# The output product's right operands, split behind FFN 1 and kept in DRAM

## The chip, the cores and the metric

The kernel is written in Bass and Tile and runs on one core of one Trainium2 chip. The metric is the device time of one execution, in microseconds; 1917.81 us is the median of three runs before the change.

## The reference

One layer of a hybrid encoder trunk, in float32, on 1024 tokens of width 1024 (weights as one would expect; D_FF is 2816):

```python
h = x + 0.5 * swiglu(rms_norm(x, ffn1_norm), w_gate1, w_up1, w_down1)      # FFN 1
z = rms_norm(h, mix_norm) @ w_in                                           # input projection
qa, ka, va, qb, kb, vb, ga, gb = split(z)
ya = neighbourhood_attention_2d(qa, ka, va, na_rpb)
yb = windowed_gqa_sink(rope(qb), rope(kb), vb, sink_logit)
merged = sigmoid(ga) * (ya @ w_branch_a) + sigmoid(gb) * (yb @ w_branch_b)
h = h + merged @ w_out                                                     # output product
h = h + 0.5 * swiglu(rms_norm(h, ffn2_norm), w_gate2, w_up2, w_down2)      # FFN 2
return rms_norm(h, final_norm)
```

The change touches two places of it: the product `merged @ w_out` (1024 x 1024 x 1024), and work that is done in the background of FFN 1.

## The kernel before

**How a product is computed.** Every float32 operand is split into a high part, a cast to fp32r on ScalarE (ACT), and a low part, the difference to that, on VectorE (DVE). One product then is three matmuls: high x high, high x low, low x high (`mm3`, L146 to 153, with a matmul in each of the lines 149, 151 and 153). The large products use Strassen's scheme in Winograd's form: seven products of half-size blocks (`PRODUCTS`, named P1 to P7) take the place of eight, at the cost of block sums and differences, which DVE forms.

**The stages**, one after the other, as the trace has them: FFN 1's gate and up products and the multiplication of the two, `hid`, until about 433 us; its down product until about 650; the input projection; both attentions and the gates until about 1160; the last part of branch A, whose results are merged; the output product from about 1196, with the next normalization at its end; FFN 2 from about 1300.

**FFN 1** (`hidden`, L429) runs 154 units of 12 matmuls, 2.72 us each. A counter `n` goes down from 153 to 0, and `behind_ffn1(n)` (L770) is called at the end of unit `n`. For a column block `i` of the hidden width the products come in the order P1, P2, P5, P6, P7, P3, P4, each for gate (m = 0) and up (m = 1). In `after` (L446), P6 is copied out of PSUM by ACT (L477, a snapshot), and P7 is then accumulated on top of it in the same bank, so P7's first matmul needs P6's copy. The results of `hid` go to DRAM on GpSimd's queue (POOL, L444).

**The background of FFN 1** is work for later stages in the gaps of ACT and DVE. A list of 28 items (8 + 8 for the branch weights, kept in `wab_d`; 12 for six gate columns, kept in `wg_d`) goes through three steps: `wab_fetch` (L749, one load of 256 KB on SyncE's queue, SP), `wab_split` (L758; cast L760, subtraction L761) and `wab_put` (L764, two transfers of 256 KB on POOL's queue, L768). One item has three units: it is fetched at n = 100 - 3i, split two units later and put one unit after that; the last one is fetched at n = 19. All of it lives in the pool `hs` (L746): six slots of 128x512. Near the end of FFN 1, `down.at_end` (L607) starts the loads for the down product: block B11 of W_down at n = 10, the left operands at 7, block B21 at 6.

**The class `Down`** (L532) runs the two down products and the output product. Its entries are (product, p), for the output product 7 x 4 = 28, each of 12 matmuls. `prep` (L579) makes an entry's operands: the left one from DRAM or from `merged`, and the right one from blocks B11, B12, B21, B22 of the weight, which it combines in place (L590 to 595: one subtraction for P5 and P3, two for P6), and it splits both. The operands lie in a ring of slots: four pairs of the pool `ws` and, in the output product, two pairs in `ar` group 2 (`ring=(8, 10)`); `prep_until(e + RING)` runs ahead by up to six entries. The blocks of w_out, eight loads of 512 KB, are loaded by `load_blocks` in the loop over branch A's last part, at every second step.

**What sets the order.** Each engine has one queue in order. A scheduler orders each engine's instructions by priority when the program is built. Those that are marked with `pin` (`tc.keep_in_program_order`) keep the order in which they are written; the background's casts and subtractions are pinned, so are the casts of the output product (`late=True`).

Of the kernel before, what the change touches and what calls it, by code (L numbers as in the profile page):

```python
# [10 lines left out]
F32 = mybir.dt.float32  # L11
F32R = mybir.dt.float32r
AF = mybir.ActivationFunctionType
ALU = mybir.AluOpType

P = 128
T = 1024
D = 1024
NC8 = D // P
# [12 lines left out]
def f32v(ap):  # L32
    return ap.bitcast(F32)


@with_exitstack
def trunk_kernel(ctx, tc, x, xt, n1, wg1, wu1, wd1, nm, win, rpb, sink, wa, wb, wo,
                 n2, wg2, wu2, wd2, nf, c_rope, c_mask_a, c_mask_b, out):
    nc = tc.nc

# [9 lines left out]
    dram = ctx.enter_context(tc.tile_pool(name="dram", bufs=1, space=bass.MemoryType.DRAM))  # L50
# [3 lines left out]
    def nm_(s):  # L54
        uid[0] += 1
        return f"{s}_{uid[0]}"
# [16 lines left out]
    def new_ar(g, dt=F32R):  # L73
        ar[g] = main.tile([P, 4, 1024], dt, tag=f"ar{g}", bufs=1, name=nm_("ar"))
        return ar[g]

    def slot(k):
        return ar[k // 4][:, k % 4, :]
# [10 lines left out]
    def ws4():  # L89
        return main.tile([P, 1024], F32R, tag="ws", bufs=8, name=nm_("ws"))  # L90

    pin = tc.keep_in_program_order

    def split(dst_hi, dst_lo, src, eng=None, late=False):
        hi = nc.scalar.copy(dst_hi, src)  # L95
        if late:
            pin(hi)
        (eng or nc.vector).tensor_tensor(dst_lo, src, f32v(dst_hi), op=ALU.subtract)  # L98
# [56 lines left out]
    def drain(gen, n=1 << 30):  # L155

        for _ in range(n):
            if next(gen, gen) is gen:
                return

    def res(t):

        return fx[t] if t < 4 else fa[:, (t - 4) * 1024:(t - 3) * 1024]
# [23 lines left out]
    B11, B21, T2, T1, B22, T3, T4 = range(7)  # L187
# [47 lines left out]
    PRODUCTS = ("P1", "P2", "P5", "P6", "P7", "P3", "P4")  # L235
    RIGHT = dict(P1=B11, P2=B21, P6=T2, P5=T1, P7=T3, P3=B22, P4=T4)

    def products(src, n, after, at_end, extra, ring, by_hand=False, last=PRODUCTS, early_rooms=(), swapped=None):
# [144 lines left out]
        def prep_until(n):  # L383
            while done[0] < min(n, len(seq)):
                prep(done[0])
                done[0] += 1
# [135 lines left out]
    def pair_slots(s):  # L522
        return slot(s), slot(s + 1)
# [5 lines left out]

    SOURCE = dict(P1="B11", P2="B21", P5="B11", P6="B11", P3="B22", P7="B12", P4="B21")  # L530

    class Down:  # L532
# [2 lines left out]

        ORDER = ("P2", "P1", "P5", "P6", "P3", "P7", "P4")

        def __init__(self, n, w, scale, place, left=None, dram=None, loads={}, ring=(22, 24, 26), shift=0, late=False):
            self.n, self.w, self.scale, self.place, self.left, self.dram, self.loads = n, w, scale, place, left, dram, loads
            self.seq = [(k, p) for k in self.ORDER for p in range(n)]  # L540
            self.dk = [k for k in self.ORDER if k in dram]
            self.nd = (n + 1) // 2
            self.raw, self.nraw, self.done, self.ent, self.tiles, self.loaded = {}, 0, 0, {}, {}, {}
            self.TAIL, self.late = min(n, 5), late
            self.ring, self.shift, self.RING = ring, shift, 4 + len(ring)
            self.W = self.Y = None
# [32 lines left out]
        def prep(self, e):  # L579
            k, p = self.seq[e]  # L580
            if k in self.dram:
                d = self.dk.index(k) * self.nd + p // 2
                self.load_left(d + 3)
                left = self.raw[d][:, p % 2, :]
            else:
                left = self.left(k, p)
            b11, b12, b21, b22 = [self.blocks(n, p)[:, 0, :] if n in self.loaded else None for n in ("B11", "B12", "B21", "B22")]
            eng = nc.gpsimd if self.n > self.RING else nc.vector
            if k == "P5":
                nc.vector.tensor_tensor(b11, b12, b11, op=ALU.subtract)  # L590
            elif k == "P6":
                nc.vector.tensor_tensor(b11, b22, b11, op=ALU.subtract)
                eng.tensor_tensor(b12, b22, b12, op=ALU.subtract)
            elif k == "P3":
                eng.tensor_tensor(b21, b21, b11, op=ALU.subtract)
            i = (e + self.shift) % self.RING
            s, t = (ws4(), ws4()) if i < 4 else pair_slots(self.ring[i - 4])
            split(s[:, :512], s[:, 512:], left, None, self.late)
            split(t[:, :512], t[:, 512:], dict(B11=b11, B12=b12, B21=b21, B22=b22)[SOURCE[k]], None, self.late)
            self.ent[e] = s, t  # L600
# [74 lines left out]
    def down_ffn(wd, src):  # L675

        place = {n: [divmod(h0 + p, 8) for p in range(NP)] for n, h0 in (("B11", 0), ("B22", NP), ("B21", NP + 7), ("B12", 2 * NP + 7))}
        place["B22"][7:] = [(f"xs{k // 2}", k % 2) for k in range(4)]
        loads = {}
        for t in range(NTT):  # L680
            loads.setdefault(2 + t, []).append(lambda d, t=t: nc.sync.dma_start(res(t), src(t)))
        for name, e0 in (("B12", 8), ("B22", 19)):
            for a in range((NP + 1) // 2):
                loads.setdefault(e0 + a, []).append(lambda d, name=name: d.load_blocks(name, 2))
        return Down(NP, wd, 0.5, place, dram={k: hid[i] for i, k in enumerate(PRODUCTS)}, loads=loads)
# [8 lines left out]
    down = down_ffn(wd1[0], lambda t: x2[t])  # L694
# [47 lines left out]
    gates = [dc for dc in [*range(8, 16), *range(8)] if 18 + dc not in sum((p for g in groups for p in g), ())]  # L742
    wg_d = dram.tile([len(gates), 2, P, 1024], F32, name="wg_d")
    cast = {}

    def hs(dt):  # L746
        return main.tile([P, 512], dt, tag="hs", bufs=6, name=nm_("hs"))
# [16 lines left out]
    def wab_put(i):  # L764
        g, half = divmod(i - 2 * NC8, 2)
        for k, a in enumerate(cast.pop(i)):
            dst = wab_d[i, :, k * 512:k * 512 + 512] if g < 0 else wg_d[g, k, :, half * 512:half * 512 + 512]
            nc.gpsimd.dma_start(dst, f32v(a))  # L768

    def behind_ffn1(n):  # L770
        down.at_end(n)
        if n <= 60 and spread:
            nc.sync.dma_start(*spread.pop(0))
        for e, f in ((3, wab_put), (2, wab_split), (0, wab_fetch)):
            i, k = divmod(100 - e - n, 3)
            if k == 0 and 0 <= i < 2 * (NC8 + len(gates)):
                f(i)

    hg = hidden(wg1, wu1, behind_ffn1, (8, 10, 9, 11), by_hand=True)


# [371 lines left out]
    for c in range(5):  # L1153
        n = 14 * (NG - 1) - 8 - 6 * c
# [111 lines left out]
    def branch_a(i):  # L1266

        bs = [bank("dg"[i % 2]) for _ in range(2)]
        a_mm.append((bs, branch_mm(bs, mix.pop(("w", NC8 + i)), Y_A)))

    def merged(dc):
        return slot((0, 1, 2, 3, 24, 25, 26, 27)[dc])
# [40 lines left out]
    def a_fetch(i):  # L1313
        mix["ra", i] = raw4()
        nc.sync.dma_start(mix["ra", i], g_d[a_order[i] * P:(a_order[i] + 1) * P, :])

    def a_open(i):
        r = mix["ra", i]
        pin(nc.scalar.activation(r, r, AF.Tanh, scale=0.5))
# [191 lines left out]
    def load_h(t):  # L1511
        nc.sync.dma_start(res(t), h_d[t * P:(t + 1) * P, :])


    left_d = dram.tile([4, 4, P, 512], F32, name="left_d")

    def quarter(k, p):
        m = merged(p + (4 if k in ("P2", "P4") else 0))
        return m[:, :512] if k in ("P1", "P2") else m[:, 512:]

    place = dict(B11=[(4, p) for p in range(4)], B21=[(4, 4 + p) for p in range(4)],
                 B12=[(1, p) for p in range(4)], B22=[(1, 4 + p) for p in range(4)])
    loads = {t: [lambda d, t=t: load_h(t)] for t in range(NTT)}
    loads[0].append(lambda d: d.load_left(2))
    down = Down(4, wo[0], 0.5, place, quarter, {k: left_d[i] for i, k in enumerate(("P5", "P6", "P3", "P7"))},
                loads, (8, 10), late=True)

    def combine(p):
        a11, a12, a22 = [quarter(k, p) for k in ("P1", "P2", "P4")]
# [7 lines left out]
    for i, dc in enumerate(a_order):  # L1537
        r = mix.pop(("ra", i))
        if i + 2 < NC8:
            a_fetch(i + 2)  # L1540
        if i >= 2:
            branch_a(i)
        if i % 2 == 0:
            down.load_blocks(("B21", "B11", "B12", "B22")[i // 2])
        if i + 3 == NC8:
            new_ar(2)
        if i + 1 == NC8:
            down.prep_until(2)
        bs, mm = a_mm[i]
        drain(mm)  # L1550
        if i + 6 < NC8:
            fetch_w(NC8 + i + 6)
        if i + 2 < NC8:
            a_open(i + 2)
        for n in range(2):
            sl = slice(n * 512, (n + 1) * 512)
            nc.vector.scalar_tensor_tensor(out=r[:, sl], in0=r[:, sl], scalar=1.0, in1=bs[n], op0=ALU.add, op1=ALU.mult)
        nc.vector.tensor_tensor(merged(dc), merged(dc), r, op=ALU.add)
        if i % 2:
            combine(i // 2)  # L1560
# [4 lines left out]
    down = down_ffn(wd2[0], lambda t: h_d[t * P:(t + 1) * P, :])  # L1565
# [22 lines left out]
    late = {}  # L1588
# [111 lines left out]
```

## Time and profile before

| | |
|---|---|
| runs | 1917.64, 1917.81, 1918.79 us (median 1917.81) |
| profiled execution | span 1915.6 us from the first to the last instruction; its time is not listed apart from the runs, so the 2.2 us from the span to the median stand for what lies around the span |
| TensorE busy | 1905.7 us, 99% of the span, at a granted clock of 0.999 |
| VectorE, ScalarE, GpSimd busy | 1451.9, 947.5, 306.5 us |
| DMA | 338.57 MB, 177 GB/s over the span |
| output product, 1200 to 1250 us | TensorE 50.00 of 50 us busy, VectorE 49.88, DMA 216 and 106 GB/s |
| end of FFN 1, 400 to 450 us | TensorE 50.00 of 50 us busy, VectorE 30.50, DMA 335 and 387 GB/s |

Each instruction of the trace has an engine, a line of the program, an operation and the tile that it writes and reads (`fx<-g` writes `fx` from the PSUM bank `g`). Idle time ahead of an instruction is put down to what ended it (`<-PE d L153`). `L149`, `L151` and `L153` are the three matmuls of one product. "DMA to landing" is the time from the issue of a transfer until its data is there.

### The profile page before, as it was taken

The numbers are of one execution on the slowest core, as the hardware profiler recorded it, in microseconds if no ns is written. First come the engines' busy times: TensorE is split into PE (matmuls) and PEld (weight loads), VectorE is DVE, ScalarE is ACT, GpSimd is POOL, SyncE is SP. The second block draws the span as 40 slices with busy tenths as digits, with TensorE's granted clock in tenths as the row PEclk, the third lists the DMA queues.
The fourth block names the chain that finished last, engine by engine and source line by source line (L and its number), as shares of the span: only waits on it lengthen the run. The fifth ranks groups of instructions, "written<-read, shape, count | busy, mean of one in ns | idle before, by whom it ended". The sixth has DMA issues, their size and how long they took to land.

```text
span 1915.6 us, 25959 instructions
## 1 busy us (share of the span) xinstructions
PE 1905.7 (99%) x9044; PEld 1597.7 (83%) x9044; DVE 1451.9 (76%) x2545; ACT 947.5 (49%) x1847; POOL 306.5 (16%) x477
## 2 busy tenths in 40 slices
PE   9999999999999999999999999999999999999998
PEld 7888888888888888898898888888888888888886
DVE  8988766668967778755887997999675566569864
ACT  7533444444446543444888983475333333344453
POOL 0012222214400112211112201010110001005111
PEclk9999999999999999999999999999999999999999
DMA  7256656677354277753648978444432323492341
GB/s 269 95 175 217 231 200 219 205 277 284 115 180 141 105 213 236 226 176 127 176 117 228 283 225 309 171 154 133 142 110 97 118 88 110 157 357 86 119 140 61
DMA packets 174211, 338.57 MB, mean 177 GB/s; under 512 B 17280, under 2 KB 79616, under 8 KB 174080
## 3 DMA queue, kind: packets, MB, share of 16 engines
q1 hardware_dynamic: 140752, 235.18, 37.5%
q0 software_dynamic: 32464, 100.69, 15.6%
q8 instruction: 71, 1.16, 0.3%
q10 hardware_dynamic: 864, 1.05, 0.2%
q14 instruction: 60, 0.49, 0.1%
HBM read 230.43 MB, written 108.19 MB: 177 GB/s over the span
## 4 chain that ended last, share of the span: by engine, by line
PE 97%; DVE 1%; DMA 1%; ACT 0%; issue 0%; POOL 0%; SPq 0%; POOLq 0%; DVEq 0%; ACTq 0%
PE g L149 18%; PE g L153 17%; PE g L151 17%; PE d L153 12%; PE d L151 12%; PE d L149 12%; PE d L1438 2%; PE g L1457 1%; PE d L1417 1%; PE g L1452 1%; PE d L1418 1%; PE d L142 1%; DVE ar L98 0%; DMA fx<-in_xt_dram 0%; DMA fx<-v_d 0%
## 5 line engine op out<-in xcount | busy, mean ns | idle before, releaser
L149 PE MATMUL g<-ar,ws 128*128 128x512 f32 x1064 | 404.6, 393 | 0.0
L151 PE MATMUL g<-ar,ws 128*128 128x512 f32 x1064 | 401.8, 390 | 0.0
L153 PE MATMUL g<-ar,ws 128*128 128x512 f32 x1064 | 400.4, 390 | 0.0
L149 PE MATMUL d<-ar,ws 128*128 128x512 f32 x728 | 281.6, 390 | 0.4 <-ACT ar L908 0.4
L151 PE MATMUL d<-ar,ws 128*128 128x512 f32 x728 | 281.1, 389 | 0.6 <-DVE ar L910 0.6
L153 PE MATMUL d<-ar,ws 128*128 128x512 f32 x728 | 281.2, 389 | 0.0
L153 PEld LDWEIGHTS g<-ar,ws 128*128 128x128 f32 x1064 | 199.6, 188 | 41.6
L151 PEld LDWEIGHTS g<-ar,ws 128*128 128x128 f32 x1064 | 199.6, 188 | 41.0
L149 PEld LDWEIGHTS g<-ar,ws 128*128 128x128 f32 x1064 | 196.6, 188 | 35.9 <-DVE fa L1030 0.3
L332 DVE TENSOR_TENSOR ws<-raw,ws 128x512 fp32r<-128x512 f32 x216 | 147.6, 688 | 92.9 <-ACT ws L325 92.0
L325 ACT CAST ws<-raw 128x512 fp32r<-128x512 f32 x216 | 132.6, 620 | 149.6 <-PE g L153 67.0
L151 PEld LDWEIGHTS d<-ar,ws 128*128 128x128 f32 x728 | 136.7, 188 | 29.8 <-DVE ar L910 1.2
L149 PEld LDWEIGHTS d<-ar,ws 128*128 128x128 f32 x728 | 136.5, 188 | 28.9 <-ACT ar L908 0.9
L153 PEld LDWEIGHTS d<-ar,ws 128*128 128x128 f32 x728 | 136.6, 188 | 28.7 <-DVE ws L332 0.5
L95 ACT CAST ws<-raw 128x512 fp32r<-128x512 f32 x98 | 61.0, 623 | 119.2 <-PE d L153 59.9
L98 DVE TENSOR_TENSOR ws<-raw,ws 128x512 fp32r<-128x512 f32 x98 | 73.2, 747 | 44.3 <-ACT ws L95 44.2
L444 POOL DMA_DIRECT2D hid<-fx x91 | 49.2, 540 | 349.6 <-DVE fx L504 221.6
L98 DVE TENSOR_TENSOR ws<-ar,ws 128x512 fp32r<-128x512 f32 x114 | 93.5, 828 | 14.6 <-ACT ws L95 14.6
L95 ACT CAST ar<-raw 128x512 fp32r<-128x512 f32 (+1 forms) x81 | 54.0, 670 | 83.5 <-PE g L151 51.5
L149 PE MATMUL g<-ws,ws 128*128 128x512 f32 x232 | 90.9, 392 | 0.0
L153 PE MATMUL g<-ws,ws 128*128 128x512 f32 x232 | 90.4, 390 | 0.0
L151 PE MATMUL g<-ws,ws 128*128 128x512 f32 x232 | 90.3, 389 | 0.0
(344 smaller groups left out, 3830.9 us busy)
## 6 DMA issues: line engine op xcount, KB each, us to landing
raw<-hid SPq DMA_DIRECT2D x70, 512.0 KB
hid<-fx POOLq DMA_DIRECT2D x91, 256.0 KB, 2.7
ar<-in_ffn_w_down_dram SPq DMA_DIRECT2D x32, 512.0 KB
raw<-in_ffn_w_up_dram SPq DMA_DIRECT2D x31, 512.0 KB
raw<-in_ffn_w_gate_dram SPq DMA_DIRECT2D x27, 512.0 KB
hid<-fa POOLq DMA_DIRECT2D x51, 256.0 KB, 2.7
ar<-zs_d POOLq DMA_DIRECT2D x48, 256.0 KB, 7.5
raw<-in_w_in_dram SPq DMA_DIRECT2D x20, 512.0 KB
```

Of the source, the lines that this page charges most:

```text
L95: hi = nc.scalar.copy(dst_hi, src)
L98: (eng or nc.vector).tensor_tensor(dst_lo, src, f32v(dst_hi), op=ALU.subtract)
L142: nc.tensor.transpose(pt[:, c * P:(c + 1) * P], xs[:, (half * 4 + c) * P:(half * 4 + c + 1) * P], ident)
L149: nc.tensor.matmul(b, lhs[0], r[0], start=first, stop=False, **kw)
L151: nc.tensor.matmul(b, lhs[0], r[1], start=False, stop=False, **kw)
L153: nc.tensor.matmul(b, lhs[1], r[0], start=False, stop=last, **kw)
L325: nc.scalar.copy(w[0][:, :512], a)
L332: nc.vector.tensor_tensor(w[0][:, 512:], a, f32v(w[0][:, :512]), op=ALU.subtract)
L444: nc.gpsimd.dma_start(hid[PRODUCTS.index(p), i], src)
L1417: nc.tensor.matmul(b[:, :nw], un["q"][s], un["kd"][s][:, k0 * P:k1 * P], start=True, stop=False)
L1418: nc.tensor.matmul(b[:, :nw], un["q"][s], un["kl"][s][:, k0 * P:k1 * P], start=False, stop=True)
L1438: nc.tensor.transpose(pt[:, i * P:(i + 1) * P], un["pr"][s][:, i * P:(i + 1) * P], ident)
```

## The change

**The right operands of the output product** are no longer made in the output product. Three new functions do it behind FFN 1, for one p at a time: `wo_fetch` loads the four blocks of w_out for this p into four slots of `hs`, `wo_split` forms the difference that a product needs, in place, and splits it into two more slots of `hs`, and `wo_put` writes both to a new DRAM tensor `wo_d` (28 x 512 KB). A round has twelve units: p = 0 starts at n = 50, p = 1 at 38, p = 2 at 26, p = 3 at 14. The seven products follow at n0 - 0, 2, 3, 5, 6, 8, 9, in the order P2, P1, P3, P5, P7, P6, P4, each put one unit behind its split. The casts and subtractions are pinned.

In `Down.prep`, an entry with `right` set loads its high and low part from there by one transfer of 512 KB (L591) and only splits the left operand. The loads of w_out in the loop over branch A are gone.

**The list of 28 items** has now two units for an item: fetched at n = 108 - 2i, split at 106 - 2i, put at 105 - 2i, so that its last item is put at n = 51.

```diff
+            if self.right is not None:
+                i = (e + self.shift) % self.RING
+                s, t = (ws4(), ws4()) if i < 4 else pair_slots(self.ring[i - 4])
+                nc.sync.dma_start(f32v(t), self.right[PRODUCTS.index(k), p])
+                split(s[:, :512], s[:, 512:], left, None, self.late)
+                self.ent[e] = s, t
+                return
...
+    wo_d = dram.tile([len(PRODUCTS), 4, P, 1024], F32, name="wo_d")
+    wo = {}
+
+    def wo_fetch(p):
+        for n, (r0, c0) in dict(B21=(4, 0), B11=(0, 0), B22=(4, 512), B12=(0, 512)).items():
+            wo[n] = hs(F32)
+            nc.sync.dma_start(wo[n], wout[0][(r0 + p) * P:(r0 + p + 1) * P, c0:c0 + 512])
+
+    def wo_split(k):
+        for d, a, b in dict(P5=(("B11", "B12", "B11"),), P7=(("B12", "B22", "B12"),), P6=(("B11", "B22", "B11"),),
+                            P4=(("B21", "B21", "B11"),)).get(k, ()):
+            pin(nc.vector.tensor_tensor(wo[d], wo[a], wo[b], op=ALU.subtract))
+        r, h, l = wo[SOURCE[k]], hs(F32R), hs(F32R)
+        pin(nc.scalar.copy(h, r))
+        pin(nc.vector.tensor_tensor(l, r, f32v(h), op=ALU.subtract))
+        cast[k] = h, l
+
+    def wo_put(k, p):
+        for n, a in enumerate(cast.pop(k)):
+            nc.gpsimd.dma_start(wo_d[PRODUCTS.index(k), p, :, n * 512:n * 512 + 512], f32v(a))
+
+    background = {}
+    for i in range(2 * (NC8 + len(gates))):
+        for e, f in ((0, wab_fetch), (2, wab_split), (3, wab_put)):
+            background.setdefault(108 - 2 * i - e, []).insert(0, (f, i))
+    for p in range(4):
+        n = 50 - 12 * p
+        background.setdefault(n, []).append((wo_fetch, p))
+        for j, k in enumerate(("P2", "P1", "P3", "P5", "P7", "P6", "P4")):
+            background.setdefault(n - 1 - 3 * (j + 1) // 2 + 1, []).append((wo_split, k))
+            background.setdefault(n - 1 - 3 * (j + 1) // 2, []).insert(0, (wo_put, k, p))
+
     def behind_ffn1(n):
         down.at_end(n)
         if n <= 60 and spread:
             nc.sync.dma_start(*spread.pop(0))
-        for e, f in ((3, wab_put), (2, wab_split), (0, wab_fetch)):
-            i, k = divmod(100 - e - n, 3)
-            if k == 0 and 0 <= i < 2 * (NC8 + len(gates)):
-                f(i)
+        for f, *a in background.get(n, ()):
+            f(*a)
...
-    place = dict(B11=[(4, p) for p in range(4)], B21=[(4, 4 + p) for p in range(4)],
-                 B12=[(1, p) for p in range(4)], B22=[(1, 4 + p) for p in range(4)])
...
-    down = Down(4, wo[0], 0.5, place, quarter, {k: left_d[i] for i, k in enumerate(("P5", "P6", "P3", "P7"))},
-                loads, (8, 10), late=True)
+    down = Down(4, None, 0.5, {}, quarter, {k: left_d[i] for i, k in enumerate(("P5", "P6", "P3", "P7"))},
+                loads, (8, 10), late=True, right=wo_d)
...
-        if i % 2 == 0:
-            down.load_blocks(("B21", "B11", "B12", "B22")[i // 2])
```

How the order of the instructions moves, at three places.

ACT in the last block of FFN 1, before the change. `d` and `g` are PSUM banks; the last two copies to `fx_75` are the snapshots of P6, and L325 makes the high parts of FFN 1's own weights:

```order
L325 CAST ws_3303<-fa 128x512
L500 ACTIVATE fa<-fa 128x512
L325 CAST ws_3331<-raw_3118 128x512
L477 COPY fa<-d_3334 128x512
L325 CAST ws_3348<-fa 128x512
L477 COPY fa<-d_3351 128x512
L325 CAST ws_3365<-raw_3120 128x512
L477 COPY fx_75<-g_3253 128x512
L95 CAST ws_3439<-raw_3381 128x512
L477 COPY fx_75<-g_3270 128x512
```

The same place after it (L791 is the cast in `wo_split`, of P1, P3, P5 and P7 with p = 3):

```order
L500 ACTIVATE fa<-fa 128x512
L791 CAST hs_3479<-hs_3415 128x512
L325 CAST ws_3518<-raw_3268 128x512
L791 CAST hs_3513<-hs_3417 128x512
L477 COPY fa<-d_3521 128x512
L325 CAST ws_3537<-fa 128x512
L477 COPY fa<-d_3540 128x512
L791 CAST hs_3555<-hs_3415 128x512
L325 CAST ws_3559<-raw_3270 128x512
L477 COPY fx_75<-g_3424 128x512
L95 CAST ws_3647<-raw_3575 128x512
L791 CAST hs_3584<-hs_3419 128x512
```

Four casts have come in between. Three of them stand ahead of P6's first snapshot, and the fourth ahead of its second (`L477 COPY fx_75<-g_3445`, the row behind the last one here).

POOL at the same place, after the change. Before it, this queue held only the puts of `hid` there (L444), since the list's last put lay further ahead:

```order
L797 DMA wo_d<-hs_3438 128x512
L797 DMA wo_d<-hs_3439 128x512
L797 DMA wo_d<-hs_3479 128x512
L797 DMA wo_d<-hs_3480 128x512
L444 DMA hid<-fa 128x512
L797 DMA wo_d<-hs_3513 128x512
L797 DMA wo_d<-hs_3514 128x512
L797 DMA wo_d<-hs_3555 128x512
```

The two puts of a product (high, low) follow each other, and one put of `hid` stands between those of P1 (3479, 3480) and P3 (3513, 3514).

SP at the start of the output product, before the change:

```order
L576 DMA raw_11129<-left_d 128x2x512
L1512 DMA fa<-h_d 128x1024 x2
L576 DMA raw_11131<-left_d 128x2x512
L576 DMA raw_11133<-left_d 128x2x512
L576 DMA raw_11206<-left_d 128x2x512
L1512 DMA fa<-h_d 128x1024 x2
```

And after it:

```order
L577 DMA raw_11334<-left_d 128x2x512
L591 DMA ws_11341<-wo_d 128x1024
L591 DMA ws_11346<-wo_d 128x1024
L1550 DMA fa<-h_d 128x1024 x2
L591 DMA ws_11370<-wo_d 128x1024
L591 DMA ws_11388<-wo_d 128x1024
L577 DMA raw_11336<-left_d 128x2x512
L577 DMA raw_11338<-left_d 128x2x512
L577 DMA raw_11405<-left_d 128x2x512
L591 DMA ws_11408<-wo_d 128x1024
```

The loads of `wo_d` stand between those of the residual (`h_d`) and of the left operands (`left_d`), one for each entry.

More of the change, by code (lines that the diff above doesn't have):

```diff
@@ L36, in trunk_kernel @@
 @with_exitstack
-def trunk_kernel(ctx, tc, x, xt, n1, wg1, wu1, wd1, nm, win, rpb, sink, wa, wb, wo,
+def trunk_kernel(ctx, tc, x, xt, n1, wg1, wu1, wd1, nm, win, rpb, sink, wa, wb, wout,
                  n2, wg2, wu2, wd2, nf, c_rope, c_mask_a, c_mask_b, out):
@@ L536, in trunk_kernel, with __init__ @@
         ORDER = ("P2", "P1", "P5", "P6", "P3", "P7", "P4")
-        def __init__(self, n, w, scale, place, left=None, dram=None, loads={}, ring=(22, 24, 26), shift=0, late=False):
+        def __init__(self, n, w, scale, place, left=None, dram=None, loads={}, ring=(22, 24, 26), shift=0, late=False, right=None):
+            self.right = right
             self.n, self.w, self.scale, self.place, self.left, self.dram, self.loads = n, w, scale, place, left, dram, loads
```

## The prediction

> **What bounds the kernel now.** I read the page first (busy times, chain), then the list of everything that TensorE waits for, then busy time by stretch.
>
> ```profile
> span 1915.6 us, 25959 instructions
> PE 1905.7 (99%) x9044; PEld 1597.7 (83%) x9044; DVE 1451.9 (76%) x2545; ACT 947.5 (49%) x1847; POOL 306.5 (16%) x477
> PE 97%; DVE 1%; DMA 1%; ACT 0%; issue 0%; POOL 0%; SPq 0%; POOLq 0%; DVEq 0%; ACTq 0%
> ...
> PE g L829 <- POOL ident masks.py:199: 1.5, 1, 1.5
> PE d L151 <- DVE ar L910: 0.6, 2, 0.3
> PE d L149 <- ACT ar L908: 0.4, 1, 0.4
> PE d L1438 <- DVE ws L98: 0.2, 1, 0.2
> ```
>
> TensorE is busy for 1905.7 of 1915.6 us and its matmuls are untouched by the change. The waits (us in total, times, longest) add up to 2.7 us in the whole program, and the first three lie in the opening stage. So nothing that only frees another engine can gain more than a fraction of a microsecond. The time can change in one way: by a new stall of TensorE. The next rows give, for each 25 us, the busy time (and instructions) of PE, PEld, DVE, ACT and POOL, then the granted clock, the busy share of the DMA engines and GB/s.
>
> ```profile
> 325.00:350.00 25.00, 25.00 (x112) 20.71 (x111) 15.76 (x25) 10.60 (x19) 4.33 (x8) 1.00 0.67 210
> 375.00:400.00 25.00, 25.00 (x112) 20.71 (x111) 17.89 (x28) 9.84 (x17) 5.40 (x10) 1.00 0.53 179
> 400.00:425.00 25.00, 25.00 (x112) 20.71 (x111) 11.48 (x18) 10.51 (x19) 1.08 (x2) 1.00 0.93 335
> 425.00:450.00 25.00, 25.00 (x112) 20.68 (x111) 19.02 (x32) 11.97 (x22) 2.70 (x5) 1.00 1.02 387
> ...
> 1200.00:1225.00 25.00, 25.00 (x111) 20.44 (x110) 24.92 (x41) 11.67 (x22) 1.72 (x4) 1.00 0.61 216
> 1225.00:1250.00 25.00, 25.00 (x112) 20.71 (x111) 24.96 (x42) 12.78 (x23) 0.00 (x0) 1.00 0.33 106
> ```
>
> Two things stand out. Behind the output product (1200 to 1250) VectorE is full, yet PE has no idle time. And at the end of FFN 1 (400 to 450) the DMA engines are full, at a share of 0.93 to 1.02, because W_down is loaded there.
>
> **The output product** loses 28 casts on ACT, 28 subtractions on DVE for the low parts, and 16 block subtractions on DVE.
>
> ```profile
> L98 DVE TENSOR_TENSOR ws<-ar,ws 128x512 fp32r<-128x512 f32 x25 | 16.5, 683 | 0.0
> L95 ACT CAST ws<-ar 128x512 fp32r<-128x512 f32 x24 | 14.1, 618 | 22.6 <-PE d L153 9.5 <-DVE ar L592 6.7 <-DVE ar L590 5.8
> ```
>
> That is 44 x 0.683 = 30 us of DVE and 28 x 0.618 = 17 us of ACT. What it is worth is read from the waits: PE's only wait on a split made there is at most the 0.2 us of the last row of that list. I put the gain at 0.1 us, between 0 and 0.2.
>
> The 28 loads of 512 KB that come instead move 0.524 MB every 2.72 us, the pitch of one entry (12 matmuls). Over the 25 us from 1200 that is 4.8 MB beside 5.4 MB (216 GB/s), some 409 GB/s, against the 387 GB/s at which the share read 1.02. So that stretch would be near its ceiling. Their cover is the ring of six pairs: a slot comes free when the entry six back has ended, which leaves 5 x 2.72 = 13.6 us for the load. A transfer of half that size took 5.4 to 7.3 us in the full stretch below; two such behind each other make 10.8 to 14.6. I take them as just hidden, at 0, and keep +3 us for the range (a lateness of 1 to 2.4 us at the first one or two turns of the ring). The eight w_out loads that go from 1140 to 1170 free DMA time where PE never waited: 0.
>
> **The list in FFN 1, packed.** It keeps its 28 items; each has one cast of 0.616, one subtraction of 0.687 and two puts of 0.540 on POOL, now in 5.44 us and not 8.16. ACT, DVE and POOL are filled to 42, 63 and 17% in the row from 325, so this is hidden: 0. A slot of the six is reused two items later, 10.9 us, against landings of 3.9 us.
>
> ```profile
> L761 DVE TENSOR_TENSOR hs<-hs,hs 128x512 fp32r<-128x512 f32 x28 | 19.2, 687 | 17.0 <-ACT hs L760 16.9
> L760 ACT CAST hs<-hs 128x512 fp32r<-128x512 f32 x28 | 17.2, 616 | 0.0
> wab_d<-hs POOLq DMA_DIRECT2D x32, 256.0 KB, 3.9
> hid<-fx POOLq DMA_DIRECT2D x32, 256.0 KB, 3.0
> ```
>
> **The four rounds of w_out behind FFN 1.** They add 28 casts (17 us ACT) and 44 subtractions (30 us DVE) over some 128 us. Those fit beside the busy times above. The wait is what counts. A round keeps its four blocks in four of the six slots, so one pair is left: the high cast of each product must wait until the put of the product before has landed in DRAM. It is pinned in ACT's queue, and behind it stand ACT's PSUM copies, which TensorE needs. I follow this in the last round, whose puts meet the W_down loads. ACT's rows there in the kernel before (start, duration, idle time before it and releaser), and PE's:
>
> ```profile
> 401.07 0.63 ACT L500 ACTIVATE fa<-fa 128x512 f32<-128x512 f32 x1
> 403.12 0.62 ACT L325 CAST ws<-raw 128x512 fp32r<-128x512 f32 x1 [1.42 <-PE d L153]
> ...
> 408.99 0.62 ACT L325 CAST ws<-raw 128x512 fp32r<-128x512 f32 x1
> 411.22 0.59 ACT L477 COPY fx<-g 128x512 f32<-128x512 f32 x1 [1.61 <-PE g L153]
> 413.94 0.59 ACT L477 COPY fx<-g 128x512 f32<-128x512 f32 x1 [1.61 <-PE g L153]
> ...
> 411.02 0.39 PE L149 MATMUL g<-ar,ws 128*128 128x512 f32 x1
> 413.74 0.39 PE L149 MATMUL g<-ar,ws 128*128 128x512 f32 x1
> ```
>
> The copies at 411.22 and 413.94 take P6's two halves out of PSUM. P7 adds into the same banks from 413.74, so P7's first half needs the first copy, with 1.9 us to spare today, and its second half, 2.72 us later, the second. In the new order the casts of P1, P3 and P5 stand ahead of the first copy, and P7's ahead of the second. How long a 256 KB put takes just there (the four rows are the puts issued from 404 to 407, 421 to 425, 427 to 430, and for comparison 300 to 395; min, median, max):
>
> ```profile
> DMA to landing us min/median/max: 6.4/6.4/6.4
> ...
> DMA to landing us min/median/max: 7.3/7.3/7.3
> ...
> DMA to landing us min/median/max: 5.4/5.5/5.5
> ...
> DMA to landing us min/median/max: 2.3/3.0/6.3
> ```
>
> The queue that fills the engines there, and the put of 6.4 us:
>
> ```profile
> 397.62 6.32 SPq L567 DMA_DIRECT2D ar<-in_ffn_w_down_dram  x6
> ...
> 405.36 0.54 POOL L444 DMA_DIRECT2D hid<-fa  x1 [9.96 <-DVE fa L504]
> ```
>
> I take 6.4 for the three puts that matter, since the first two leave in that same stretch. P1's cast follows the row at 401.07, so it ends at 401.7 + 0.6 = 402.3 and its put lands at 408.7. P3's cast ends at 409.3, its put lands at 415.7. P5's cast ends at 416.3; a cast and the first copy follow (1.1 us): 417.4. P7's first half starts there and not at 413.74: **3.7 us**. P5's put lands at 416.3 + 6.4 = 422.7; P7's cast and the second copy (1.2 us) end at 423.9, when P7's first half has been done since 420.1: **3.8 us** more. Together 7.5 us; in general the sum of the three landings less 11.7. With 5.4 each it is 4.5 us; with 7.3, 10.2; with 3.9 or less, 0. POOL's queue gives nothing back: the put of `hid` that now stands between P1's and P3's puts went out at 405.36, before P3's cast ends. The low halves on DVE follow the same pattern one put behind, and are in time.
>
> [...]
>
> **The sum**: 7.5 - 0.1, so +7.4 us on the profiled 1915.6. The median of the runs, 1917.81, lies 2.2 us above the span, as work outside of it; I add the same to it: 1917.8 + 7.4 = 1925.2 us.
>
> **The rivals.** *No stall, no change.* If the puts land within 3.9 us each, as the list's did from 160 to 395, the three waits vanish and the small gain stands: 1917.7. For it: P1's and P3's puts leave at 402.3 and about 409, and a put is small beside six loads of 512 KB. Against it: the two puts that the trace has in this stretch took 6.4 and 7.3. Chance 0.30, with any gain beyond 0.2% inside it at 0.03. [...]
>
> *The output product's loads come late.* Then, beside the stall, PE waits for `ws<-wo_d` in the first turns of the ring: 1925.2 + 3 = 1928.2. For it: 409 GB/s wanted, full ring. Against: the 13.6 us of lead, and 1225 to 1250 has room (106 GB/s). Chance 0.10.
>
> *The earlier rounds stall as well.* They have the same one pair of slots. With 5.4 us a put, each would cost 4.5, three of them 13.5: 1938.7. Against: at a DMA share of 0.53 to 0.67 the landings are 3.0 to 3.9, and the rounds add only some 48 GB/s there (4.7 MB in 32.6 us instead of 0.79 MB in 8.2). Chance 0.06.
>
> **How the numbers follow.** The last round's stall alone has 0.54, time 1925.2, its own range 1921 to 1930 (4.5 us at one end; at the other 10.2 and P2's put, which may hold P1's cast back by 1 to 2 us). For eight in ten I go from 1917.3, which takes in most of the first rival, to 1931. A measurement of this kernel tells 0.2% (3.8 us) from no change: faster 0.03; within it 0.33, the first rival and the lowest end of the forecast; slower 0.64.
>
> **What would show it.** ACT's casts from the w_out blocks should have idle time ahead of them that ends with a DMA, in the last round above all; TensorE should list two new waits on ACT's copies `fx<-g`, near 414 and 420, and the stretch 400 to 425 should hold fewer matmuls than 112. VectorE should fall from 24.9 to about 15 in the stretches of the output product, with PE as full as before. If the puts in that stretch land in 3 to 4 us, or no wait on those copies appears, my main step is wrong. If PE waits for `wo_d`, the ring of six was too short.

## The result

| | median | runs | span of the profiled execution |
|---|---|---|---|
| before | 1917.64 us | 1917.49 to 1918.79, five | 1915.6 us |
| the change | 1932.68 us | 1930.13 to 1933.69, five | 1931.9 us |

The change is slower: the ratio is 1.0075 (95% interval 1.0063 to 1.0088), some 15 us in the medians and 16.3 us in the profiled executions. The forecast was 1925.2, so the direction was right and the size half of it; 1932.68 also lies above the range's end of 1931.

The page of the changed kernel, and its list of TensorE's waits (us in total, times, longest):

```profile
span 1931.9 us, 26237 instructions
PE 1910.1 (99%) x9044; PEld 1598.2 (83%) x9044; DVE 1452.4 (75%) x2545; ACT 946.3 (49%) x1847; POOL 338.2 (18%) x533
...
PE g L149 <- ACT fx L477: 8.7, 3, 6.2
PE d L151 <- DVE ws L98: 2.3, 2, 1.8
PE g L867 <- POOL ident masks.py:199: 1.5, 1, 1.5
PE d L151 <- DVE ar L98: 1.0, 1, 1.0
PE d L151 <- DVE ar L948: 0.6, 2, 0.3
PE d L1476 <- DVE ws L98: 0.5, 2, 0.3
```

Three waits on ACT's copies of P6 are new. Two of them, in the last round, were foretold; the third, near 375 us, was not, and neither were three on DVE's splits (`L98`, in the first down product). Where all 16.3 us went can be summed from the starts of the matmuls: for each, the time to the next start less the usual pitch of its size (0.227 us at 512 columns). Against the kernel before:

| place in the changed kernel | loss, us | what it is |
|---|---|---|
| near 375 us | 1.7 | P7 waits for P6's first copy, in the third round of w_out |
| near 415 us | 6.4 | P7 waits for P6's first copy, in the last round |
| 421.9 to 424.9 us | 1.4 | matmuls at half pace behind that wait |
| near 426 us | 1.3 | P7's second half waits for the second copy |
| 509 to 537 us | 5.4 | the first down product waits for DVE's splits |
| rest | 0.1 | |

**The last round**, in the rows that answer to the prediction's. ACT (start, duration, idle time and releaser), DVE at its end, three puts on GpSimd's queue (the last of the round before, and the high halves of P1 and P3), PE, and the stretches with the granted clock:

```profile
401.66 0.62 ACT L791 CAST hs<-hs 128x512 fp32r<-128x512 f32 x1 [3.16 <-DVE ws L332]
...
406.29 0.62 ACT L791 CAST hs<-hs 128x512 fp32r<-128x512 f32 x1 [0.88 <-DMA wo_d<-hs]
...
412.84 0.62 ACT L791 CAST hs<-hs 128x512 fp32r<-128x512 f32 x1 [5.41 <-DVE ws L332]
...
420.24 0.62 ACT L791 CAST hs<-hs 128x512 fp32r<-128x512 f32 x1 [5.29 <-DMA wo_d<-hs]
...
421.29 0.58 ACT L477 COPY fx<-g 128x512 f32<-128x512 f32 x1
...
426.07 0.62 ACT L791 CAST hs<-hs 128x512 fp32r<-128x512 f32 x1 [3.69 <-DVE hs L789]
426.60 0.58 ACT L477 COPY fx<-g 128x512 f32<-128x512 f32 x1
...
424.10 0.69 DVE L792 TENSOR_TENSOR hs<-hs,hs 128x512 fp32r<-128x512 f32 x1 [4.55 <-DMA wo_d<-hs]
...
425.31 0.69 DVE L789 TENSOR_TENSOR hs<-hs,hs 128x512 f32<-128x512 f32 x1
...
397.13 0.54 POOL L797 DMA_DIRECT2D wo_d<-hs  x1 [0.72 <-ACT hs L791]
...
407.20 0.55 POOL L797 DMA_DIRECT2D wo_d<-hs  x1 [2.83 <-ACT hs L791]
...
414.27 0.54 POOL L797 DMA_DIRECT2D wo_d<-hs  x1
...
415.29 0.39 PE L153 MATMUL g<-ar,ws 128*128 128x512 f32 x1
421.92 0.79 PE L149 MATMUL g<-ar,ws 128*128 128x512 f32 x1 [6.24 <-ACT fx L477]
422.51 0.63 PE L151 MATMUL g<-ar,ws 128*128 128x512 f32 x1
...
427.23 0.50 PE L149 MATMUL g<-ar,ws 128*128 128x512 f32 x1 [1.00 <-ACT fx L477]
...
416.00:420.00 4.00, 0.00 (x0) 0.00 (x0) 1.89 (x3) 0.00 (x0) 0.54 (x1) 0.74 1.04 408
420.00:424.00 4.00, 2.08 (x5) 1.70 (x6) 0.00 (x0) 2.14 (x4) 0.54 (x1) 0.50 0.92 354
```

The five casts are those of P2, P1, P3, P5 and P7. The first four begin as the put ahead of them lands (the profile names a DVE instruction for P2's and P3's, but the puts issued at 397.13 and 407.20 us took 4.5 and 5.6 us): ACT sits idle for some 5 us ahead of P3's and P5's, and the copy at 421.29 comes right behind P5's. TensorE starts P7 0.05 us after that copy ends, and its clock has meanwhile fallen to 0.50. P7's cast waits for something else, the block subtraction at 425.31 on DVE. That one stands behind P5's low half (424.10), which waited for the put of P3's low half.

**The first down product.** GpSimd subtracts some of the blocks of W_down there (L593 of the kernel before, L601 of the changed one). Its first such rows, in the kernel before and in the changed one, with DVE's rows beside the latter:

```profile
457.00 7.84 POOL L593 TENSOR_TENSOR ar<-ar,ar 128x512 f32<-128x512 f32 x5 [23.58 <-DMA raw<-hid]
468.34 6.99 POOL L593 TENSOR_TENSOR ar<-ar,ar 128x512 f32<-128x512 f32 x2 [3.50 <-DVE ar L590]
```

```profile
478.75 16.38 POOL L601 TENSOR_TENSOR ar<-ar,ar 128x512 f32<-128x512 f32 x7 [30.49 <-DMA ar<-in_ffn_w_down_dram]
...
482.48 0.69 DVE L98 TENSOR_TENSOR ar<-raw,ar 128x512 fp32r<-128x512 f32 x1
...
485.39 1.77 DVE L98 TENSOR_TENSOR ws<-raw,ws 128x512 fp32r<-128x512 f32 x1
487.09 1.78 DVE L98 TENSOR_TENSOR ws<-ar,ws 128x512 fp32r<-128x512 f32 x1
```

They begin 21.8 us later by the clock, while FFN 1 ended some 11 us later: GpSimd waited for W_down. And they now run in one stretch of 16.4 us. From 483.80 us on, DVE's subtractions beside them take 1.67 to 1.78 us in place of 0.69. In the kernel before, TensorE waited for none of DVE's splits there; here DVE runs out of lead, and from 509 to 537 us TensorE waits for it.

**The output product** came out as forecast. These are rows of the changed kernel (as in the prediction: PE, PEld, DVE, ACT, POOL, clock, DMA share, GB/s):

```profile
1215.00:1240.00 25.00, 25.00 (x112) 20.67 (x112) 15.02 (x24) 7.22 (x13) 1.62 (x3) 1.00 1.00 385
1240.00:1265.00 25.00, 25.00 (x112) 20.71 (x111) 12.20 (x19) 5.57 (x9) 0.00 (x0) 1.00 0.87 312
```

DVE fell from 24.9 to 15.0 and 12.2 us of 25. The loads fill the DMA engines to a share of 1.00, 385 GB/s, and TensorE waits for none of them. Its late time in that stage (from 1195 to 1330 us by the clock of the kernel before) is 0.45 us, and was 0.64.

### The profile page after: what moved, and what is told of

The parts are those of the page before. It is cut to its first block, busy times and chain, and to the rows that moved or that the text cites. A ratio compares the mean times of both kernels' runs of the same rounds, so it can differ in the third digit from the quotient of the medians.

```text
span 1931.9 us, 26237 instructions
## 1 busy us (share of the span) xinstructions
PE 1910.1 (99%) x9044; PEld 1598.2 (83%) x9044; DVE 1452.4 (75%) x2545; ACT 946.3 (49%) x1847; POOL 338.2 (18%) x533
## 4 chain that ended last, share of the span: by engine, by line
PE 83%; issue 7%; DVE 4%; POOL 3%; DMA 2%; ACT 1%; POOLq 0%; SPq 0%; DVEq 0%; ACTq 0%
PE g L149 15%; PE g L151 15%; PE g L153 15%; PE d L153 10%; PE d L151 10%; PE d L149 10%; PE d L1476 2%; POOL wo_d L797 1%; DVE ws L98 1%; PE g L1495 1%; DVE ar L98 1%; PE d L1455 1%; PE d L1456 1%; PE g L1490 1%; POOL hid L444 1%
## 5 line engine op out<-in xcount | busy, mean ns | idle before, releaser
L325 ACT CAST ws<-raw 128x512 fp32r<-128x512 f32 x216 | 132.5, 619 | 136.9 <-PE g L153 59.1
L98 DVE TENSOR_TENSOR ws<-raw,ws 128x512 fp32r<-128x512 f32 x98 | 73.8, 755 | 46.3 <-ACT ws L95 46.3
L444 POOL DMA_DIRECT2D hid<-fx x91 | 49.1, 540 | 330.5 <-DVE fx L504 218.7
L98 DVE TENSOR_TENSOR ws<-ar,ws 128x512 fp32r<-128x512 f32 x94 | 79.5, 846 | 12.9 <-ACT ws L95 12.8
```

Of the source, the lines that this page charges most:

```text
L325: nc.scalar.copy(w[0][:, :512], a)
L444: nc.gpsimd.dma_start(hid[PRODUCTS.index(p), i], src)
```

## The experiments

The theory after the result: (1) the single pair of slots chains cast to put to cast, and ACT's queue carries that to TensorE; (2) the loss in the first down product has a cause of its own. The rivals: the closer list, the puts' traffic, or the output product. Losses are summed as above, matmul by matmul against the kernel before, and parted at the matmul that starts there at 445 us. FFN 1's own last matmul starts at 430 us, so the first of the two columns takes in the opening of the first down product. Times are medians beside those of the kernel before on the same chip, with the ratio's interval.

| run | time, before | ratio | lost until 445 us | lost from 445 to 650 us |
|---|---|---|---|---|
| the change | 1932.68, 1917.64 | 1.0063 to 1.0088 | 10.9 | 5.4 |
| closer list alone | 1918.27, 1918.27 | 0.9992 to 1.0011 | 0 | 0 |
| no last round | 1922.91, 1918.27 | 1.0013 to 1.0032 | 1.4 | 3.2 |
| puts without casts | 1917.49, 1918.27 | 0.9986 to 1.0005 | 0 | 0 |
| all 14 units earlier | 1930.21, 1918.27 | 1.0048 to 1.0078 | 14.7 | 0 |
| residual loaded later | 1932.51, 1918.34 | 1.0055 to 1.0089 | 11.3 | 3.8 |
| blocks subtracted on DVE | 1928.66, 1918.34 | 1.0041 to 1.0071 | 11.6 | 0 |
| high casts on GpSimd | 1939.94, 1918.34 | 1.0098 to 1.0128 | 16.2 | 7.1 |
| two pairs of slots | 1925.53, 1917.90 | 1.0024 to 1.0052 | 1.5 | 6.1 |
| two pairs, blocks on DVE | 1919.53, 1917.90 | 0.9999 to 1.0018 | 1.9 | 0 |
| before, blocks on DVE | 1918.36, 1917.90 | 0.9992 to 1.0010 | 0 | 0 |
| two pairs, SP reordered | 1919.76, 1918.05 | 1.0000 to 1.0019 | 2.2 | 0 |
| two pairs, residual later | 1922.94, 1918.31 | 1.0013 to 1.0032 | 3.2 | 2.2 |

**The closer list alone.** The kernel before, with

```diff
-        for e, f in ((3, wab_put), (2, wab_split), (0, wab_fetch)):
-            i, k = divmod(100 - e - n, 3)
-            if k == 0 and 0 <= i < 2 * (NC8 + len(gates)):
-                f(i)
+        for f, *a in background.get(n, ()):       # fetch at 108 - 2i, split at 106 - 2i, put at 105 - 2i
+            f(*a)
```

> The kernel before with one part of the change alone: the list of 28 items takes two units an item, nothing of w_out is moved. If the slot chain of the w_out rounds is the cause, as I hold, the time is that of before, 1917.6 us, and TensorE waits for no copy of FFN 1. If the closer list itself delays ACT's copies (the loss of 1.6 us near 375 us), it is 1919 or more.

It costs nothing, so the loss near 375 us belongs to the rounds too.

**No last round.**

```diff
-    for p in range(4):
+    for p in range(3):
         n = 50 - 12 * p
...
-                nc.sync.dma_start(f32v(t), self.right[PRODUCTS.index(k), p])
+                nc.sync.dma_start(f32v(t), self.right[PRODUCTS.index(k), min(p, 2)])
```

> The change without its last round (p = 3): its blocks are neither fetched nor split nor put, and the output product reads the operands of p = 2 a second time, so its result is another and its instructions and loads are the same in number and size. If the last round alone, in the stretch where W_down is loaded, makes both the stall near 415 us (9 us with the slow clock behind it) and the loss in the first down product (5.4 us), the time is near 1919.3: only the 1.7 us near 375 stay. If the output product's loads or the rounds as such cost the time, it stays near 1930.

The last round's stall in FFN 1 is gone and the third round's stays, at 1.4 us. But the first down product still loses 3.2 us, which I had tied to the last round alone. So its loss is not a mere sequel of the stall.

**Puts without casts.** The closer list, and

```diff
+    still_d = dram.tile([14, P, 512], F32, name="still_d")
+    still = {}
+    def still_make():
+        still[0] = hs(F32)
+        nc.gpsimd.memset(still[0], 0.0)
+    def still_put(j):
+        for k in range(2):
+            nc.gpsimd.dma_start(still_d[2 * j + k], still[0])
+    background.setdefault(16, []).append((still_make,))
+    for j in range(7):
+        background.setdefault(14 - 1 - 3 * (j + 1) // 2, []).insert(0, (still_put, j))
```

> The kernel before with the closer list, and with fourteen puts of 256 KB from one slot that is never rewritten, at the points where the last round has its puts. No cast or subtraction is added and nothing waits for these puts. If it is the slots' chain that stalls FFN 1, TensorE has no wait there. If the bytes alone make W_down and the left operands late for the first down product, that product loses some 5 us and the time is near 1923; if its loss comes from the chain or from the order of the queues, the time is 1917.6.

Nothing is lost, in FFN 1 or behind it. But the run does not test what it was made for. These puts are not pinned, and the trace has all fourteen of them some 100 us ahead of the stretch in which W_down is loaded:

```profile
L784 POOL DMA_DIRECT2D still_d<-hs x14: 539/542/551, 292.0 to 304.6; - x14
```

So it shows only that 3.7 MB of puts there cost nothing when nothing waits for them. Whether the puts' traffic beside W_down's loads costs time is answered by the runs with two pairs of slots below.

**All 14 units earlier.**

```diff
-            background.setdefault(108 - 2 * i - e, []).insert(0, (f, i))
+            background.setdefault(122 - 2 * i - e, []).insert(0, (f, i))
...
-        n = 50 - 12 * p
+        n = 64 - 12 * p
```

> The change with its whole background 14 units earlier, which is one column block of FFN 1: every cast keeps its place between the copies of the same products, but the last round's puts fall ahead of the W_down loads. By the slot chain with puts of 3 to 4 us the sum of three landings less 11.7 us is 0 to 0.3, and the first down product has its loads as in before: 1917.5 to 1919.5, the upper end if the loss of 1.6 us of the third round stays. If the chain stalls TensorE wherever it stands, the time stays above 1925.

The time came out above 1925, but not for the reason that went with it: the list now collided with the start of FFN 1. TensorE's waits in this run:

```profile
PE g L149 <- DVE fx L479: 6.8, 1, 6.8
PE g L149 <- ACT fa L477: 1.6, 1, 1.6
...
PE g L149 <- ACT fx L477: 1.1, 2, 0.7
PE g L149 <- DVE fa L479: 1.0, 1, 1.0
```

The waits on L479, near 133 and 159 us, come from the list: FFN 1's first blocks use slots of hs themselves (the trace shows DVE writing hs from PSUM there, L482), and I read it that the list, with fewer slots left, waited for its own puts there; this was not tried by itself. It cost 11.1 us with the slow clock behind the longer wait. The part that answers the question is the rest: the last round, out of the W_down loads but at the same place between the copies, lost 1.7 us (0.95 and 0.75, near 390 us), where it had lost 6.4 and 1.3. The third round lost 1.9, about as before (1.7). And the first down product lost nothing.

**The residual loaded later.** In the change one load of the residual held SP's queue from 446.0 to 452.3 us.

```diff
-            loads.setdefault(2 + t, []).append(...)
+            loads.setdefault(2 + t if t < 4 else 10 + t, []).append(...)
```

> The change with one reordering: in the down products the residual's tiles 4 to 7, which are needed only at the end of P5, are loaded twelve entries later, so that they no longer stand ahead of W_down's blocks and of left operands on SP's queue. In the change one such load held SP from 446.0 to 452.3 us, waiting for the last puts of hid. If that held-up queue is what the first down product loses 5.4 us to, the loss falls to 0 to 1 and the time is near 1927.5. If W_down itself comes late for another reason, or DVE is slow because GpSimd subtracts at the same time, the loss stays at 4 or more and the time near 1932.

Nearer to the second case, at 3.8 us. Six loads of W_down now go out together at 441.75 us, but the next left operand then waits by itself, for the last puts of hid, until 454.03, with the rest of W_down behind it on SP's queue until 467.89. So the residual's loads are not all that holds this queue.

**Blocks subtracted on DVE.**

```diff
-            eng = nc.gpsimd if self.n > self.RING else nc.vector
+            eng = nc.vector
```

> The change with the block subtractions of both down products on DVE and none on GpSimd. In the traces a DVE subtraction takes 0.69 us alone and 1.67 to 1.78 us while GpSimd subtracts. If the first down product loses its 5.4 us because GpSimd's late subtractions slow DVE where it has no lead left, the loss falls to 0 to 1 and the time is near 1927.5. If late operands alone are the reason, the loss stays near 5 and the time near 1932.

As expected for the overlap: the first down product loses nothing, and FFN 1 loses as much as before (11.6 us and 10.9). DVE's groups by tile in this run, from 445 to 545 us (min, median, max in ns):

```profile
L98 DVE TENSOR_TENSOR ws<-ar,ws x23: 675/679/687, 447.8 to 543.8; 128x512 fp32r<-128x512 f32 x23
L98 DVE TENSOR_TENSOR ar<-ar,ar x17: 674/678/685, 446.6 to 538.1; 128x512 fp32r<-128x512 f32 x17
L601 DVE TENSOR_TENSOR ar<-ar,ar x7: 678/679/680, 483.6 to 496.0; 128x512 f32<-128x512 f32 x7
```

DVE does 22 subtractions more in that time, and none takes over 0.69 us. The same edit on the kernel **before** changes nothing, since TensorE did not wait there:

> The kernel before with the block subtractions of both down products on DVE and none on GpSimd. TensorE waits for nothing in the first down product of the kernel before, so by my reading the time stays at 1917.6 to 1918.5 and only DVE's subtractions there take 0.69 us each. If the overlap costs time in every kernel, not only where the operands are late, it is 1916.5 or less.

**High casts on GpSimd.**

```diff
-        pin(nc.scalar.copy(h, r))
+        pin(nc.gpsimd.tensor_copy(h, r))
```

> The change with the high casts of the four rounds on GpSimd instead of ACT; the low subtractions stay on DVE, the slots and their waits stay. If ACT's queue carries the wait to TensorE, the copies of P6 come in time, the loss in FFN 1 falls from 10.9 us to 0 to 2, and the time is 1922 to 1924 with the first down product's loss left. If DVE's queue, where the low halves wait in the same way, carries it too, TensorE waits for DVE in its place and the time stays at 1928 or more.

The second case held, and more: with ACT free, DVE's queue carried the wait.

```profile
PE g L149 <- DVE fa L497: 9.6, 2, 9.3
PE d L151 <- DVE ws L98: 3.1, 3, 1.8
PE g L149 <- DVE fx L497: 2.4, 2, 1.8
```

The low subtraction of a product waits for a slot just as the high cast does, and behind it on DVE stand the sums (L497) that empty PSUM for the next product. Moving one half of the chain to another engine moved the wait.

**Two pairs of slots.**

```diff
-        r, h, l = wo[SOURCE[k]], hs(F32R), hs(F32R)
+        if k in ("P1", "P5", "P6"):
+            g = const.tile([P, 1152], F32R, tag="gain", bufs=1, name=nm_("pair"))
+            r, h, l = wo[SOURCE[k]], g[:, :512], g[:, 512:1024]
+        else:
+            r, h, l = wo[SOURCE[k]], hs(F32R), hs(F32R)
```

> The change with a second pair of slots for the rounds of w_out: the high and low halves of P1, P5 and P6 go into the tile of the norm's gain, which is idle there, and those of the other products stay in hs. Casts, subtractions, puts and their order of issue are the same in number. If the single pair of slots is what makes each cast wait for the put before it and so stalls FFN 1, its loss falls from 10.9 us to 0 to 2 and the time is 1918 to 1924, the upper end with the first down product's loss left as it is. If the traffic of the puts or ACT's load is the cause, the loss stays near 10 and the time near 1932.

The chain is shown. ACT's rows at the place of the stall, in this run:

```profile
401.63 0.62 ACT L795 CAST hs<-hs 128x512 fp32r<-128x512 f32 x1 [0.38 <-DMA wo_d<-hs]
402.69 0.60 ACT L795 CAST pair<-hs 128x512 fp32r<-128x512 f32 x1
...
411.98 0.62 ACT L795 CAST pair<-hs 128x512 fp32r<-128x512 f32 x1 [2.61 <-DMA wo_d<-pair]
413.03 0.57 ACT L477 COPY fx<-g 128x512 f32<-128x512 f32 x1
414.57 0.62 ACT L795 CAST hs<-hs 128x512 fp32r<-128x512 f32 x1 [0.96 <-DVE hs L789]
415.62 0.57 ACT L477 COPY fx<-g 128x512 f32<-128x512 f32 x1
...
400.00:425.00 25.00, 25.00 (x112) 20.73 (x111) 12.12 (x19) 9.62 (x17) 6.00 (x12) 1.00 1.02 371
```

With the same casts and puts, P6's copies start at 413.0 and 415.6 and not at 421.3 and 426.6, and TensorE is full although the DMA share is 1.02. The last round's fourteen puts went out from 398.5 to 432.5 us here, so their traffic is not what stalled FFN 1. FFN 1 itself now loses nothing: the 1.5 us of the table lie behind its last matmul, near 432 and 440 us, and are waits on DVE. The first down product still loses 6.1 us with no stall ahead of it, so that loss has a cause of its own.

**Two pairs, and the blocks on DVE.** Both edits:

> Both remedies in one: the second pair of slots, and the block subtractions of the down products on DVE. If the slots' chain and the overlap of GpSimd's and DVE's subtractions are all that the change costs, what is left is the kernel before less 0 to 0.2 us: 1917.4 to 1919, the same as before. If the output product's loads cost something that the stalls have hidden so far, the time is above 1920.

Of the change's 15 us, 1.6 are left, and the interval takes in no change. So the output product's loads hide no cost.

**Two pairs, SP's queue reordered.** GpSimd subtracts again; the loads are moved:

```diff
-            loads.setdefault(2 + t, []).append(...)
+            loads.setdefault(2 + t if t < 4 else 20 + t, []).append(...)
...
         for e, f in ((2, bias_fetch), (5, bias_add), (10, bias_put)):
-            k = e + 6 * h
+            k = e + 6 * h + 14
```

> The change with the second pair of slots (FFN 1 no longer stalls), GpSimd subtracting as before, and on SP's queue W_down's blocks and the left operands ahead of the residual's tiles 4 to 7 (22 entries later) and of the background of the bias (14 entries later). The order by which the change's schedule places the blocks of W_down behind loads that wait was the last difference left to the kernel before. If that order makes GpSimd's subtractions late and so pushes them onto DVE's busy stretch, the first down product's loss falls from 6.1 us to 0 to 1.5 and the time is 1919 to 1921. If the blocks come late for lack of bandwidth, the loss stays near 6 and the time near 1925.5.

The loss behind 445 us is gone. The first of GpSimd's subtractions with two pairs of slots, without the reordering and with it:

```profile
469.01 17.71 POOL L601 TENSOR_TENSOR ar<-ar,ar 128x512 f32<-128x512 f32 x7 [28.73 <-DMA ar<-in_ffn_w_down_dram]
```

```profile
459.66 7.83 POOL L601 TENSOR_TENSOR ar<-ar,ar 128x512 f32<-128x512 f32 x5 [18.79 <-DMA ar<-in_ffn_w_down_dram]
```

It is issue order, not bandwidth, that made W_down late. SP's rows for W_down show it: without the reordering one transfer at 430.98 and the next only at 450.54, with it six from 430.48.

```profile
430.98 0.43 SPq L568 DMA_DIRECT2D ar<-in_ffn_w_down_dram  x1
450.54 0.91 SPq L568 DMA_DIRECT2D ar<-in_ffn_w_down_dram  x2
```

```profile
430.48 3.23 SPq L568 DMA_DIRECT2D ar<-in_ffn_w_down_dram  x6
451.28 0.94 SPq L568 DMA_DIRECT2D ar<-in_ffn_w_down_dram  x2
```

**Two pairs, the residual alone later** (the first of the two edits above):

> As the run before it, with only the residual's tiles 4 to 7 moved 22 entries later; the loads of the bias's background keep their place ahead of W_down's blocks. If the residual's loads, which wait for the last puts of hid, were what held the queue, the first down product's loss stays at 0 to 1 us and the time is 1919 to 1920.5. If the masks, which wait for slots of hs, held it as well, some of the 6 us come back and the time is 1921 to 1925.

It leaves 2.2 of the 6.1 us. Both groups of loads held W_down back: GpSimd's first subtraction starts at 469.01 us with neither moved, at 464.46 with the residual's later and at 459.66 with both. The second edit also moves the bias's additions on DVE (L732) to later, so its share of the 2.2 us is not shown to be the queue's alone. Over all runs in which GpSimd subtracts, the loss follows that start. Counted from 457.0 us, and less what was lost until then, it is 0 to 0.4 us late where nothing is lost (all 14 units earlier; SP reordered), 4.3 us where 2.2 are lost, 6.0 (no last round) and 8.0 (residual later) where 3.2 and 3.8 are, and 9.9 to 10.9 where 5.4 to 7.1 are. No version beat the kernel before.

## Why the prediction was wrong

*What bounds the kernel, and the gain.* Right. The output product gave 0.2 us, where I had said 0.1 between 0 and 0.2; DVE's relief went to no one.

*The stall of the last round.* Right in mechanism and place, and 7.6 us against the 7.5 of the sum. But this hides errors that cancelled, and the agreement is luck. The chain reached P1's cast some 3 us late: with the third round's 1.7 us added, the sum has it at 403.4, and it came at 406.3. P2's cast had waited for the last put of the round before, which left at 397.13 us; I had put P2's own lateness at 1 to 2 us, at the range's end. Against that, the second wait shrank from 3.8 to 1.2 us: P7's cast came 5.8 us behind P5's and not 7.0, and P7's first half, at half pace, covered another 1.4 us. And it was not P5's put that held P7's cast, as the sum has it. SP had nothing to issue from 414.9 to 425.4 us, and this put landed in 3.0 us, at 424.75; by it alone the cast would have been in time. The cast came at 426.07, behind DVE's chain of low halves, of which I had said that they are in time. From P1's cast to P5's it was 13.95 us, and 14.0 in the sum, but from other parts: the two puts landed in 5.6 and 5.9 us and not 6.4, and they left 0.9 and 1.4 us behind the start of their casts and not 0.6.

*The clock.* No term stood for it: 1.4 us.

*The earlier rounds.* I gave a rival 0.06 by which all three would stall for 4.5 us each. One did, for 1.7 us. Against the rival I had set landings of 3.0 to 3.9 us; in the middle they were even shorter (2.5 us from 330 to 370 us, 2.8 from 370 to 397). But the rounds run into each other without slack. The second round's last put, issued at 360.49 us beside the third round's four loads of w_out (from 359.60), took 7.1 us, and the third round's first cast waited for it until 367.69.

*The first down product.* This is the step that failed. My sum had no term for it: I took W_down's loads only as a burden on the puts, and never asked what in the new order of SP's queue would come late behind FFN 1. Within the 16.3 us it is 5.4, the largest of the three terms that the sum lacks (the clock's 1.4 and the third round's 1.7 are the others). In the changed kernel SP issues loads of masks (437.82 us) and of the residual (442.08 and 452.30) ahead of W_down's next blocks (444.81 and 452.72); the order of SP's queue that I had shown is that of the output product alone. Without this loss the time would have been near 1927, inside the range.

*The rivals.* "No stall" failed at 10.9 us: it asked for puts that land within 3.9 us, and P1's and P3's took 5.6 and 6.0 us (from issue to the next cast); only P2's and P5's, at 3.6 and 3.0, were as short. "The output product's loads come late" failed: share 1.00, and no wait.

## What to carry to other kernels

Before background work is put into a pinned queue, follow each slot round its whole circle, cast, put, landing, next cast, and set that time against the gap between the copies that stand behind it; one more pair of slots took FFN 1's loss of 10.9 us away here, all but 1.5 us that came up behind it, and moving the cast to another engine made it worse. Do the same for the second engine that works on those slots: here DVE's low halves held up a cast on ACT. When a queue's order changes, read it to the end of the next stage as well: W_down's blocks came late because loads that wait were put ahead of them, not for want of bandwidth. And a long stall can cost more than its length: behind the waits of 6.2 and 6.8 us TensorE restarted at half pace here, which cost 1.4 and 2.7 us more.

## What the runs showed of the hardware

TensorE's clock fell to 0.50 behind the wait of 6.2 us, and the next six matmuls took 0.43 to 0.59 us each from start to start in place of 0.227: 1.4 us on top. In the run with everything 14 units earlier, 13 matmuls did so behind a wait of 6.8 us (2.7 us; the granted clock from 160 to 175 us was 0.66); no such row follows the wait of 1.6 us in that run, nor those of 1.47 and 1.76 us in the change (until 377.28 and 529.17 us). With the high casts on GpSimd, though, eight matmuls from 537.08 us on took 0.42 to 0.43 us each, 1 us behind a wait of 1.8 us, and no run here says why.

A DVE subtraction of 128x512 took 0.68 us without GpSimd's and up to 1.79 us beside them, in the kernel before too. It was not slower from the start of GpSimd's rows: in the change the row begins at 478.75 us and DVE's subtractions still take 0.69 us until 483.8, and in the kernel before the row at 468.34 us has DVE at 0.68 until 472.5. No run shows why. One of DVE's groups in the kernel before, from 445 to 545 us (min, median, max in ns):

```profile
L98 DVE TENSOR_TENSOR ar<-ar,ar x17: 677/687/1782, 444.9 to 542.8; 128x512 fp32r<-128x512 f32 x17
```

It cost time only where DVE had no lead: with the blocks on DVE the kernel before stays the same (1918.36 us, 1917.90), and the changed one gets back 5.4 us.
